# Joint logits of the two key kinds in half of the first attention, with later yields, a later lambda and another raw copy

## The chip, the cores and the metric

The kernel runs on one core of a Trainium2 chip. The metric is the device time of one execution in microseconds (us). The kernel before takes 1781.61 us (median of three runs, 1781.35 to 1781.64). The core has five engines that work in parallel: TensorE (PE; its weight loads are the row PEld), VectorE (DVE), ScalarE (ACT), GpSimd (POOL) and SyncE (SP, which issues most DMAs). Each takes its own instructions strictly in the order in which the program issued them; semaphores make one wait for another. Matmul results land in PSUM, in banks of 128 x 512 fp32.

## The reference

A trunk of two layers, sequence 512, model width 1024, fp32. Cut to what the change touches:

```python
q_rot = rope(q, positions); k_slc = rope(k_slc, positions); k_win = rope(k_win, positions)
def block(i):                                   # 128 queries
    logit_c = einsum('btghd,bngd->bghtn', qg, kc) * scale      # compressed keys, unrotated q
    p_c = masked_softmax(logit_c, cmp_end <= t)
    logit_s = einsum('btghd,bgtkd->bghtk', qrg, ks) * scale    # "selected" keys
    p_s = masked_softmax(logit_s, kpos <= t)
    logit_w = einsum('btghd,bkgd->bghtk', qrg, kw) * scale     # "window" keys
    p_w = masked_softmax(logit_w, mask_w)
    return gb[..., 0:1] * (p_c @ vc) + gb[..., 1:2] * (p_s @ vs) + gb[..., 2:3] * (p_w @ vw)
lam = exp(sum(lq1 * lk1)) - exp(sum(lq2 * lk2)) + lambda_init  # for the second, differential attention
h = rmsnorm(x); proj = h @ w_in                                # the dense part, and so on to the FFN
```

With 512 positions, 16 selected blocks of 64 and a window of 512, both the selected and the window attention come to plain causal attention, each with its own keys and values. The first attention has 8 heads of width 64 in two groups g; a group shares its keys. The second (differential) attention needs the scalar `lam`; a gMLP (`sgu`) is the third mixer. All three are merged by gates, and an FFN follows.

## The kernel before

**The dense products** (input projection, merge, FFN) are the bulk of PE's work. Each fp32 product is made as three products of split operands (high x high, low x high, high x low), L184 to L186 with 512 columns each, or L224 to L226 in the token-major form `tm`. Weights arrive by DMA; ACT rounds them to the high part (L163, `wh`), DVE or POOL subtracts for the low part (L166, `wl`). Every dense chunk takes one of three PSUM banks `g`, and the next chunk but two must wait until the evacuation of that bank has ended.

**The small work** (aux work) is woven in. `layer_tasks` lists the dense tasks, `aux_tasks` two lanes of generators: lane X with `tables` (sines and cosines, and before the change the lambdas too), `cmp_aux` (compression MLP), `sgu_aux` and `cmp_soft` (softmax over compressed keys, for g = 0 and 1, parts A and B), lane Y with `nsa` (first attention) and `diff` (second). In `run`, each dense step yields a cost in ns; a lane gets that much credit and `step` runs it to its next yield, which charges its own price. So a larger yielded number sets everything behind it later in program order, on every engine's queue at once. `later(n, f)` sets f back by n such steps; `D_OA` holds the three delays of the first attention's output: the sum `fin` (L963), the rounding `hi_` (ACT, L969) and the low part `lo_` (L972). The program is fixed when it is built; nothing moves at run time.

**The first attention**, `nsa(g)`, goes over 32 units: pairs of heads hp, halves of the queries, key kinds (0 selected, 1 window), query tile i of the half, head h. For each unit `sA` makes logits in one of two banks `s` (`logits`, L871 and L872: high and low part of the keys, (i+1)*128 columns), DVE masks and takes the row maximum (L860), ACT exponentiates (L862). `sN` normalises (DVE L898, POOL L902), `sB` transposes on PE into one of two banks `t` (L919), ACT and DVE split the result (L920, L928), `sC` multiplies with the values (L941) into bank `o`. The rotated keys of all four (kind, g) pairs lie in `KR`, two tiles, one for a kind.

**Rotary embedding** of the queries (`rope_pair`): the halves of a projection are multiplied out of PSUM by DVE (L659, L660 and L669, L670), and for `QA0`, `QA1` a raw copy is kept for the compressed attention (ACT, L664 and L672). Only when the last reader has ended does the bank come free. After `QA1` the values `V` follow in the dense order (L224 to L226 with 280 columns).

Of the kernel before, what the change touches and what calls it, by code (L numbers as in the profile page):

```python
# [15 lines left out]
AF = mybir.ActivationFunctionType  # L16
# [5 lines left out]
P, TT, KT, FT = 128, 4, 8, 22  # L22
# [3 lines left out]
QA, KC, VC, KS, VS, KW, VW, GA, QB, KB, VB, UU, VV = (  # L26
    0, 512, 640, 768, 896, 1024, 1152, 1280, 1304, 1816, 2328, 2840, 3352)
# [3 lines left out]
D_ROPE = (1500, 3500, 11000, 18000, 24000, 33000)  # L31
D_MX, D_ACT, D_OA, D_XP = (2, 4), (7, 19), (1, 4, 17), 2
D_NORM = (10, 13)
# [47 lines left out]
class Kern:  # L81
# [287 lines left out]
    def setup2(self):  # L369

        nc = self.nc
# [13 lines left out]
        for j in range(2):  # L385
            a = sm(f"a{j}")
# [10 lines left out]
        c = 1 / (2 * pi)  # L397
        cs = []
        e = 18
        for _ in range(4):  # L400
            q = Fraction(int(c * 2 ** e), 2 ** e)
# [4 lines left out]
        k = sm("k")  # L406
        f = sm("f")
# [23 lines left out]
        for j, off in enumerate((0.25, 0.0)):  # L431
            w = sm("w")
# [5 lines left out]
            d = sm("d")  # L438
# [6 lines left out]
        for j, tab in enumerate((self.cosT, self.sinT)):  # L445
            for h in range(4):
                nc.sync.dma_start(tab[32 * h:32 * h + 32, :], tab_d[j].rearrange("a b c -> a (b c)"))
        yield
        first = len(nc.cur_bb.bb.instructions)
        lq = self.lq.rearrange("p (l f d) -> p l f d", l=L, f=4)  # L450
        self.nlam, self.bh, self.sub = [], [], []
        for l in range(L):
            li = 0.8 - 0.6 * math.exp(-0.3 * l)
            ex = self.const(f"ex{l}", [P, 2])
# [15 lines left out]
        self.holds.append((first, len(nc.cur_bb.bb.instructions)))  # L470
        yield

# [123 lines left out]
    def cmp_aux(self, which):  # L596
        nc = self.nc
        ps = self.hid[which]
# [5 lines left out]
        nc.scalar.activation(hg[0:64], hg[0:64], AF.Gelu_apprx_tanh)  # L604
        yield 4500
        pt = self.bank("t", [P, 2, 64])
# [4 lines left out]
        if which == "k":  # L611
# [4 lines left out]
            for ab in range(2):  # L616
                for k in range(2):
                    c0 = (k * 2 + ab) * P
                    nc.tensor.matmul(pk[:, ab, :], w2[:, c0:c0 + P], hT[:, k, :],
                                     start=(k == 0), stop=(k == 1))  # L620
# [31 lines left out]
    def rope_pair(self, name, raw=None):  # L652
# [13 lines left out]
        def fb(ps):  # L666
# [4 lines left out]
            if raw is not None:  # L671
                nc.scalar.activation(st["raw"][:, 1, :], ps, AF.Copy)  # L672
            o1, o2 = st["t1"], st["t4"]
# [62 lines left out]
    def sgu_aux(self):  # L736
# [40 lines left out]
        norm(0)  # L777
        yield 650
        pss, tmps = {}, {}
# [14 lines left out]
    def cmp_soft(self, g, part):  # L794
# [54 lines left out]

        for w, f in (((1300, s0), (1300, s1), (2600, s2), (2600, ex)), ((2600, s3), (2600, s4), (1300, s5)))[part]:  # L850
            f()
            yield w
# [12 lines left out]
    def logits(self, q, k, kl, i):  # L865

        nc = self.nc
        n = (i + 1) * P
        ts = slice(i * P, (i + 1) * P)
        s = self.bank("s")  # L870
        nc.tensor.matmul(s[:, :n], q[:, ts], k[:, :n], start=True, stop=False)  # L871
        nc.tensor.matmul(s[:, :n], q[:, ts], kl[:, :n], start=False, stop=True)  # L872
        return s

    def nsa(self, g):
# [3 lines left out]
        units = [(2 * hp + h, half, kind, 2 * half + ii) for hp in range(2) for half in range(2)  # L879
                 for kind in range(2) for ii in range(2) for h in range(2)]  # L880
        E, PT, OB, LO = {}, {}, {}, []
        st = {}

        def sA(u):
            hh, half, kind, i = units[u]
            s = self.logits(q2[hh // 2][:, hh % 2], kh[kind][:, g], kl[kind][:, g], i)
            if u % 2 == 0:
                st["sm"] = self.small("sm2", 2, 5)
            E[u] = self.soft(s, (i + 1) * P, i, st["sm"][:, u % 2:u % 2 + 1])[0], st["sm"]
# [109 lines left out]
    def diff(self, p):  # L999
# [6 lines left out]
        def sA(u, j):  # L1006
            c, i = units[u]
            s = self.logits(q2[c][:, j], kh[c][:, j], kl[c][:, j], i)
            E[u, j] = self.soft(s, (i + 1) * P, i)
# [132 lines left out]
    def merge_tasks(self, add, l, br, first, last, need, lead=1):  # L1142
        def gate(i0, m):
            if last and m == 0:
                for c in range(4):
                    self.load_x(self.xsrc, c)
            yield from self.fm(i0, [self.gate_evac(br, m)], self.xg)

        def branch(i0, m):
            x = {"a": self.oa, "b": self.ob, "c": self.oc}[br]  # L1150
            yield from self.fm(i0, [self.br_evac(br, m, first, last)], x, K=4)
            if m == 7 and last:
                self.ensure("mx")
        B = br.upper()
        for m in range(8 + lead):
            if m < 8:
                add("g%s%d" % (B, m), [("g" + br, m)], lambda i0, m=m: gate(i0, m))
            if m >= lead:
                add("b%s%d" % (B, m - lead), [("b" + br, m - lead)], lambda i0, m=m: branch(i0, m - lead), need=need)
# [142 lines left out]
    def layer_tasks(self, l):  # L1302
# [103 lines left out]
        add("V", [("v", c) for c in range(3)], g_v)  # L1406
        self.merge_tasks(add, l, "c", True, False, ["sgu"])
        add("KB0", [("KB0", "A"), ("KB0", "B")], g_rope("KB0"), need=["rows1"])
# [34 lines left out]
    def aux_tasks(self, l):  # L1443
# [7 lines left out]
        X.append(("sgu", ["vv%d" % l], self.sgu_aux))  # L1451
        X.append(("softA0", ["QA0%d" % l], lambda: self.cmp_soft(0, 0)))
        X.append(("cmpv", ["wv3%d" % l], lambda: self.cmp_aux("v")))
        X.append(("softB0", ["V%d" % l], lambda: self.cmp_soft(0, 1)))
# [17 lines left out]
    def run(self):  # L1472
# [3 lines left out]
        lanes = [[], []]  # L1476
        tag = lambda n, l: n if n == "tables" else n + str(l)
        for l in range(L):
# [57 lines left out]
def pack(inp):  # L1536
# [9 lines left out]
    for l in range(L):  # L1546
        w = w_in[l]
        groups = {"KR": [KS, KS + 64, KW, KW + 64]}
        for g in range(2):
# [89 lines left out]
```

## Time and profile before

| | |
|---|---|
| median of three runs | 1781.61 us |
| profiled execution | 1781.37 us |
| its span (first to last instruction) | 1779.6 us |
| PE busy | 1761.8 us (99%), 8500 matmuls |
| PEld, DVE, ACT, POOL busy | 83%, 54%, 42%, 20% |
| PE's longest waits in total | ACT raw 2.2, DVE nm 1.9, ACT hg 1.9, POOL e 1.2 us |

About 1.8 us of the profiled execution lie outside its span. A busy PE is not a PE at its best pace: the end of a matmul is modelled, so its cost in a stream is read as the distance from its start to the next start. The order of the instructions on each engine comes from the program and not from the trace.

### The profile page before, as it was taken

What the parts mean: (1) busy time and instruction counts of PE and PEld (TensorE: products, weight loads), DVE (VectorE), ACT (ScalarE), POOL (GpSimd) and SP (SyncE); (2) the same over time, 40 slices, a digit from 0 to 9 for tenths busy, and PEclk for the clock granted to TensorE, in tenths of its full rate; (3) what the DMA queues carried; (4) which work ended last, traced back from release to release, by engine and by line L of the source; (5) the groups of instructions that cost most, each with busy time, mean ns of one, the idle gap of its engine ahead of it and who ended that gap; (6) DMA issues with size and microseconds to landing.
All of it is one profiled execution on the core that took longest, in us unless ns stands there. A gap on an engine that the chain in (4) does not pass through costs nothing. (4 is left out here: it accounts for less than half of the span.)

```text
span 1779.6 us, 22826 instructions
## 1 busy us (share of the span) xinstructions
PE 1761.8 (99%) x8500; PEld 1470.8 (83%) x8500; DVE 968.7 (54%) x1772; ACT 752.9 (42%) x1320; POOL 352.4 (20%) x355
## 2 busy tenths in 40 slices
PE   9999999999999999999999999999999999999998
PEld 7888888888888888888888888888888888888887
DVE  6786674665644444433366676746656444444222
ACT  6456673444433332222234576634444332332222
POOL 0234331444120000000012343315440200000000
PEclk9999999999999999999999999999999999999999
DMA  7571116532222222223344711165323232222221
GB/s 260 180 224 69 54 60 195 172 107 100 105 104 92 98 95 95 95 102 124 106 147 139 222 42 60 69 191 156 141 71 110 92 109 102 97 95 95 95 102 52
DMA packets 67726, 205.78 MB, mean 116 GB/s; under 512 B 8992, under 2 KB 9376, under 8 KB 67616
## 3 DMA queue, kind: packets, MB, share of 16 engines
q1 hardware_dynamic: 67472, 204.29, 34.0%
q8 instruction: 67, 1.10, 0.2%
q14 instruction: 43, 0.35, 0.1%
q10 hardware_dynamic: 144, 0.04, 0.0%
HBM read 185.29 MB, written 19.01 MB: 115 GB/s over the span
## 5 line engine op out<-in xcount | busy, mean ns | idle before, releaser
L163 ACT ACTIVATE wh<-wr 128x1024 fp32r<-128x1024 f32 (+2 forms) x320 | 315.4, 989 | 658.6 <-PE ps_g L186 355.8
L184 PE MATMUL ps_g<-xg,wh 128*128 128x512 f32 x1400 | 555.9, 397 | 0.2
L185 PE MATMUL ps_g<-xg,wl 128*128 128x512 f32 x1400 | 546.2, 390 | 0.3 <-DVE wl L166 0.3
L186 PE MATMUL ps_g<-xg,wh 128*128 128x512 f32 x1400 | 546.4, 390 | 0.1
L166 DVE TENSOR_TENSOR wl<-wr,wh 128x1024 fp32r<-128x1024 f32 (+1 forms) x308 | 366.0, 1190 | 238.0 <-ACT wh L163 237.3
L186 PEld LDWEIGHTS ps_g<-xg,wh 128*128 128x128 f32 x1400 | 262.8, 188 | 56.5 <-DVE xg L283 1.0
L185 PEld LDWEIGHTS ps_g<-xg,wl 128*128 128x128 f32 x1400 | 263.4, 188 | 48.6 <-DVE wl L166 0.6
L184 PEld LDWEIGHTS ps_g<-xg,wh 128*128 128x128 f32 x1400 | 263.1, 188 | 48.9 <-ACT xg L280 1.0
L862 ACT ACTIVATE e<-e,nm 128x128 f32<-128x128 f32 (+1 forms) x192 | 107.5, 560 | 102.3 <-DVE nm L860 95.3
L184 PE MATMUL ps_g<-act,wh 128*128 128x512 f32 (+1 forms) x374 | 141.2, 378 | 0.0
L185 PE MATMUL ps_g<-act,wl 128*128 128x512 f32 (+1 forms) x374 | 140.8, 376 | 0.0
L186 PE MATMUL ps_g<-act,wh 128*128 128x512 f32 (+1 forms) x374 | 140.8, 376 | 0.0
L493 POOL TENSOR_TENSOR acc<-acc,sq 128x512 f32<-128x512 f32 x18 | 29.3, 1629 | 433.6 <-ACT sq L492 433.6
L860 DVE CUSTOM_DVE_ANT_0 e<-ps_s,con 128x128 f32<-128x128 f32 (+1 forms) x192 | 92.2, 483 | 26.6 <-PE ps_s L872 21.9
L902 POOL TENSOR_SCALAR e<-e,sm,ga 128x256 f32<-128x256 f32 (+3 forms) x128 | 82.0, 653 | 119.6 <-DVE sm L898 107.3
L1184 DVE TENSOR_TENSOR fb<-ps_g,R 128x512 f32<-128x512 f32 x44 | 30.4, 692 | 129.1 <-PE ps_g L186 129.1
L166 POOL TENSOR_TENSOR wl<-wr,wh 128x512 fp32r<-128x512 f32 x48 | 73.4, 1530 | 118.8 <-ACT wh L163 118.8
L1175 DVE TENSOR_TENSOR fa<-ps_g,R 128x512 f32<-128x512 f32 x44 | 30.4, 692 | 95.3 <-PE ps_g L186 95.3
L184 PEld LDWEIGHTS ps_g<-act,wh 128*128 128x128 f32 x374 | 70.3, 188 | 13.0
L186 PEld LDWEIGHTS ps_g<-act,wh 128*128 128x128 f32 x374 | 70.3, 188 | 13.0
L185 PEld LDWEIGHTS ps_g<-act,wl 128*128 128x128 f32 x374 | 70.4, 188 | 12.7
L1227 POOL TENSOR_TENSOR acc<-acc,sq 128x512 f32<-128x512 f32 x5 | 6.9, 1382 | 316.6 <-ACT sq L1225 316.6
(248 smaller groups left out, 2548.1 us busy)
## 6 DMA issues: line engine op xcount, KB each, us to landing
wr<-in_wst SPq DMA_DIRECT2D x266, 512.0 KB, 3.3
rp_d<-pc SPq DMA_DIRECT2D x112, 128.0 KB, 3.4
wr<-in_wst SPq DMA_DIRECT2D x52, 256.0 KB, 2.6
q<-rp_d SPq DMA_DIRECT2D x16, 512.0 KB, 5.5
kh<-rp_d SPq DMA_DIRECT2D x24, 256.0 KB, 6.0
xT<-in_xT SPq DMA_DIRECT2D x7, 512.0 KB, 5.8
kl<-rp_d SPq DMA_DIRECT2D x12, 256.0 KB, 6.9
xtok<-in_xtok SPq DMA_DIRECT2D x4, 512.0 KB, 8.8
```

The lines of the kernel that those rows point to most:

```text
L163: nc.scalar.activation(h[:, :w], t[:, :w], AF.Copy)
L166: eng.tensor_tensor(lo[:, a:b], t[:, a:b], h[:, a:b].bitcast(F32), op=OP.subtract)
L184: nc.tensor.matmul(out, wh[:, c], xh[:, ts], start=first, stop=False)
L185: nc.tensor.matmul(out, wl[:, c], xh[:, ts], start=False, stop=False)
L186: nc.tensor.matmul(out, wh[:, c], xl[:, ts], start=False, stop=last)
L493: (nc.vector if k == KT - 1 else nc.gpsimd).tensor_tensor(self.acc, self.acc, sq, op=OP.add)
L860: nc.vector.tensor_tensor_reduce(out=e[:, :n], in0=s[:, :n], in1=self.mask[:, S - n:], scale=-0.125, scalar=3e38, op0=OP.add, op1=OP.min, ...
L862: nc.scalar.activation(e[:, :n], e[:, :n], AF.Exp, bias=nm, scale=-1.0, accum_out=sm)
L902: nc.gpsimd.tensor_scalar(e[:, :n], e[:, :n], sm[:, h:h + 1], self.ga[:, i, b:b + 1], op0=OP.mult, op1=OP.mult)
L1175: self.nc.vector.tensor_tensor(t, ps, self.R, op=OP.mult)
L1184: nc.vector.tensor_tensor(t, ps, self.R, op=OP.mult)
L1227: (nc.vector if k == KT - 2 else nc.gpsimd).tensor_tensor(self.acc[:, ts], self.acc[:, ts], sq[:, ts], op=OP.add)
```

## The change

It has four parts.

- **Joint logits.** The columns of `KR` are put in another order, so that one tile holds both kinds of one group. For half 0 (query tiles 0 and 1) one pair of products covers both kinds: 256 columns instead of two pairs of 128 for tile 0, 512 instead of two pairs of 256 for tile 1. The second kind's softmax reads the other half of the same bank later. In half 0 the units run kind by kind within a tile. Over two layers and two groups, 32 pairs of 128 columns and 32 of 256 become 16 of 256 and 16 of 512: 64 matmuls fewer. Half 1 is as it was.
- **Later traces.** `D_OA` goes from (1, 4, 17) to (3, 6, 17); `cmp_aux` for the keys of layer 0 yields 6500 instead of 4500 before its transposes; `sgu_aux` yields 1950 instead of 650 after its first norm; `cmp_soft` of group 0 gets an empty first stage of 2600, and its `s2` yields 1300 instead of 2600.
- **Lambda order.** The lambdas leave `tables` and become an aux task of their own behind `softA0`; gate tasks no longer wait for the mixer, and the merge of mixer c also needs the lambdas.
- **Raw copy.** The second raw copy of `QA1` is made by DVE instead of ACT.

```diff
-D_MX, D_ACT, D_OA, D_XP = (2, 4), (7, 19), (1, 4, 17), 2
+D_MX, D_ACT, D_OA, D_XP = (2, 4), (7, 19), (3, 6, 17), 2
...
+    def lambdas(self):
...
-        yield
+        yield 300
...
-        yield 4500
+        yield 6500 if which == "k" and self.l == 0 else 4500
...
             if raw is not None:
-                nc.scalar.activation(st["raw"][:, 1, :], ps, AF.Copy)
+                if raw == 0:
+                    nc.scalar.activation(st["raw"][:, 1, :], ps, AF.Copy)
+                else:
+                    nc.vector.tensor_copy(st["raw"][:, 1, :], ps)
...
         norm(0)
-        yield 650
+        yield 1950
...
-        for w, f in (((1300, s0), (1300, s1), (2600, s2), (2600, ex)), ((2600, s3), (2600, s4), (1300, s5)))[part]:
+        for w, f in (((2600 * (g == 0), lambda: None), (1300, s0), (1300, s1), (1300, s2), (2600, ex)), ((2600, s3), (2600, s4), (1300, s5)))[part]:
...
-        n = (i + 1) * P
         ts = slice(i * P, (i + 1) * P)
         s = self.bank("s")
-        nc.tensor.matmul(s[:, :n], q[:, ts], k[:, :n], start=True, stop=False)
-        nc.tensor.matmul(s[:, :n], q[:, ts], kl[:, :n], start=False, stop=True)
+        o = s[:, :(i + 1) * P] if len(k.shape) == 2 else s[:, :2 * (i + 1) * P].rearrange("p (a n) -> p a n", a=2)
+        nc.tensor.matmul(o, q[:, ts], k, start=True, stop=False)
+        nc.tensor.matmul(o, q[:, ts], kl, start=False, stop=True)
         return s
...
-                 for kind in range(2) for ii in range(2) for h in range(2)]
+                 for kind, ii in ([(0, 0), (1, 0), (0, 1), (1, 1)], [(0, 0), (0, 1), (1, 0), (1, 1)])[half]
+                 for h in range(2)]
...
-            s = self.logits(q2[hh // 2][:, hh % 2], kh[kind][:, g], kl[kind][:, g], i)
+            if half:
+                s = self.logits(q, kh[g][:, kind, :n], kl[g][:, kind, :n], i)
+            elif kind == 0:
+                s = self.logits(q, kh[g][:, :, :n], kl[g][:, :, :n], i)
+                st["s", u % 2] = s[:, n:]
+            else:
+                s = st["s", u % 2]
...
-                add("g%s%d" % (B, m), [("g" + br, m)], lambda i0, m=m: gate(i0, m))
+                add("g%s%d" % (B, m), [("g" + br, m)], lambda i0, m=m: gate(i0, m), need=need[1:])
...
-        self.merge_tasks(add, l, "c", True, False, ["sgu"])
+        self.merge_tasks(add, l, "c", True, False, ["sgu", "lambda"])
...
         X.append(("softA0", ["QA0%d" % l], lambda: self.cmp_soft(0, 0)))
+        if l == 0:
+            X.append(("lambda", [], self.lambdas))
...
-        groups = {"KR": [KS, KS + 64, KW, KW + 64]}
+        groups = {"KR": [KS, KW, KS + 64, KW + 64]}
```

In the program after, a line behind the inserted code has a higher number than in the program before: the `hg` activation L604 is L608 there, the two exponentials L460 are L464, the softmax step L860 is L867, the sum L963 is L980.

**ACT, layer 0, around the first compression MLP.** `ang` is the argument of the sine tables, `ex` the lambdas' exponentials, `ctmp` and `hg` the hidden layer of the MLP, which PE then transposes. Before:

```order
L441 ACT_TABLE_LOAD
L441 ACTIVATE ang<-ang 128x128 x2
L460 ACT_TABLE_LOAD
L460 ACTIVATE ex_600<-ex_600 128x2
L460 ACTIVATE ex_611<-ex_611 128x2
L600 ACTIVATE ctmp<-ps_s 64x256
L163 ACTIVATE wh<-wr 128x1024
L604 ACT_TABLE_LOAD
L604 ACTIVATE hg<-hg 64x256
```

After:

```order
L604 ACTIVATE ctmp<-ps_s 64x256
L441 ACT_TABLE_LOAD
L441 ACTIVATE ang<-ang 128x128 x2
L608 ACT_TABLE_LOAD
L608 ACTIVATE hg<-hg 64x256
L163 ACTIVATE wh<-wr 128x1024
```

`ctmp` stands ahead of the sines now, and the exponentials with their table load are gone from in front of `hg`. On PE the two transposes that read `hg` stand five dense products later than before.

**DVE, layer 0, end of `QA1`'s evacuation** (`t` products of the rotation, `raw` the raw copy, `hg` the other compression MLP). Before:

```order
L660 TENSOR_TENSOR t_1061<-ps_g,sinR 128x512
L603 TENSOR_TENSOR hg<-ps_s,ctmp 64x256
L166 TENSOR_TENSOR wl<-wr,wh 128x840
L669 TENSOR_TENSOR t_1123<-ps_g,sinR 128x512
L670 TENSOR_TENSOR t_1124<-ps_g,cosR 128x512
L166 TENSOR_TENSOR wl<-wr,wh 128x840
```

After (the last of the fourteen lambda rows that stand between L166 and L673):

```order
L469 TENSOR_SCALAR bh_1096<-par_64 128x24
L472 TENSOR_SCALAR sub_1098<-par_64 128x1
L461 ISA junk,ex_1089<-lq 128x64
L461 ISA ex_1089 128x1
L466 SCALAR_TENSOR_TENSOR nl_1083<-ex_1078 128x1
L466 SCALAR_TENSOR_TENSOR nl_1094<-ex_1089 128x1
L673 TENSOR_TENSOR t_1120<-ps_g,sinR 128x512
L674 TENSOR_TENSOR t_1121<-ps_g,cosR 128x512
L679 COPY raw<-ps_g 128x512
L607 TENSOR_TENSOR hg<-ps_s,ctmp 64x256
```

The lambdas' fourteen DVE instructions, two of which wait for ACT's exponentials, moved in front of the three readers of `QA1`'s bank; `hg` moved behind them. In layer 1 the same place holds no lambda.

**DVE, first attention of group 0, start of the half with tiles 2 and 3** (`ce`, `cmx`, `csm` belong to the compressed softmax of group 1, `oa` to the output of an earlier pair of heads). Before:

```order
L822 TENSOR_TENSOR ce<-ce,cmx 128x512
L860 ISA e,nm<-ps_s,con 128x256
L860 ISA nm 128x1
L830 TENSOR_REDUCE csm<-ce 128x16
L831 RECIPROCAL csm<-csm 128x16
L963 TENSOR_TENSOR oa<-oa,otmp 128x512
L898 RECIPROCAL sm_1805<-sm_1805 128x2
L834 TENSOR_TENSOR csm<-csm,ga 128x16
L836 TENSOR_TENSOR csm<-csm,con 128x16
L928 TENSOR_TENSOR pt<-ps_t,pt 128x4x128
L860 ISA e,nm<-ps_s,con 128x384
L860 ISA nm 128x1
```

After:

```order
L829 TENSOR_TENSOR ce<-ce,cmx 128x512
L980 TENSOR_TENSOR oa<-oa,otmp 128x512
L945 TENSOR_TENSOR pt<-ps_t,pt 128x2x128
L867 ISA e,nm<-ps_s,con 128x384
L867 ISA nm 128x1
L989 TENSOR_TENSOR oa<-oa 128x512
L837 TENSOR_REDUCE csm<-ce 128x16
L867 ISA e,nm<-ps_s,con 128x384
L867 ISA nm 128x1
L838 RECIPROCAL csm<-csm 128x16
```

The first softmax step of 384 columns stood behind six other instructions after the reduction over `ce`; now it stands ahead of that reduction.

## Rows read from the trace of the kernel before

**Rows 1.** Page, busy time (share of the span) and instructions of PE
```profile
PE 1761.8 (99%) x8500; PEld 1470.8 (83%) x8500; DVE 968.7 (54%) x1772; ACT 752.9 (42%) x1320; POOL 352.4 (20%) x355
```
**Rows 2.** Waits of PE: line, releaser; us in total, times, longest
```profile
PE ps_g L224 <- ACT raw L672: 2.2, 2, 1.1
PE ps_s L871 <- DVE nm L860: 1.9, 2, 0.9
PE ps_t L608 <- ACT hg L604: 1.9, 1, 1.9
...
PE ps_t L919 <- POOL e L902: 1.2, 2, 0.6
...
PE ps_t L805 <- ACT raw L672: 0.9, 2, 0.6
...
PE ps_s L757 <- DVE v L752: 0.3, 1, 0.3
```
**Rows 3.** Timeline of PE, pair of 128 columns: start, us, instruction [idle <-releaser]
```profile
130.43 0.22 PE L871 MATMUL ps_s<-kh,q 128*128 128x128 f32 x1
...
130.60 0.45 PE L184 MATMUL ps_g<-xg,wh 128*128 128x512 f32 x1
130.88 0.39 PE L185 MATMUL ps_g<-xg,wl 128*128 128x512 f32 x1
```
**Rows 4.** Timeline of PE, a pair of 256, then a pair of 512
```profile
172.75 0.28 PE L871 MATMUL ps_s<-kh,q 128*128 128x256 f32 x1
...
173.00 0.40 PE L184 MATMUL ps_g<-xg,wh 128*128 128x512 f32 x1
173.23 0.40 PE L185 MATMUL ps_g<-xg,wl 128*128 128x512 f32 x1
...
250.60 0.40 PE L871 MATMUL ps_s<-kh,q 128*128 128x512 f32 x1
...
251.06 0.49 PE L919 MATMUL ps_t<-con,e 128*128 128x128 f32 x3
```
**Rows 5.** Groups of PE by line and shape: xcount, busy us, mean ns
```profile
L941 PE MATMUL ps_o<-pt,v 128*128 128x256 f32 x64 | 12.7, 280 | 0.0
```
**Rows 6.** Timeline of PE at the transposes of `hg`, layer 0
```profile
66.70 0.35 PE L608 MATMUL ps_t<-con,hg 64*128 64x64 f32 x2 [1.86 <-ACT hg L604]
```
**Rows 7.** Windows: from:to, length, busy (x count), granted PE clock, DMA
```profile
66.90:70.40 3.50, 3.50 (x10) 2.74 (x9) 0.29 (x1) 1.73 (x3) 1.84 (x2) 0.51 0.60 177
118.00:119.50 1.50, 1.47 (x10) 1.33 (x10) 1.50 (x1) 0.21 (x1) 1.44 (x2) 1.00 0.70 234
```
**Rows 8.** Timeline of ACT ahead of `hg`, layer 0
```profile
61.64 0.31 ACT L441 ACTIVATE ang<-ang 128x128 f32<-128x128 f32 x1 [0.73 <-DVE ang L440]
61.97 1.28 ACT L460 ACT_TABLE_LOAD   x1
63.27 0.30 ACT L460 ACTIVATE ex<-ex 128x2 f32<-128x2 f32 x2
```
**Rows 9.** Timeline of PE, ACT and DVE at `V`'s third bank, layer 0
```profile
118.03 0.40 PE L224 MATMUL ps_g<-wh,xg 128*128 128x280 f32 x1 [1.11 <-ACT raw L672]
...
117.40 0.57 ACT L672 ACTIVATE raw<-ps_g 128x512 f32<-128x512 f32 x1
...
113.58 0.42 DVE L603 TENSOR_TENSOR hg<-ps_s,ctmp 64x256 f32<-64x256 f32 x1 [1.25 <-ACT ctmp L600]
...
115.33 0.68 DVE L669 TENSOR_TENSOR t<-ps_g,sinR 128x512 f32<-128x512 f32 x1
115.93 0.68 DVE L670 TENSOR_TENSOR t<-ps_g,cosR 128x512 f32<-128x512 f32 x1
```
**Rows 10.** Timeline of DVE, the first lambda instruction
```profile
60.20 0.22 DVE L457 CUSTOM_DVE_ANT_0 junk<-lq 128x64 f32<-128x64 f32 x1
```
**Rows 11.** Timeline of DVE and PE, first attention, start of tiles 2 and 3
```profile
176.46 0.69 DVE L963 TENSOR_TENSOR oa<-oa,otmp 128x512 f32<-128x512 f32 x1 [0.47 <-ACT otmp L960]
...
178.93 0.50 PE L871 MATMUL ps_s<-kh,q 128*128 128x512 f32 x1 [0.93 <-DVE nm L860]
```

More of the change, by code (lines that the diff above doesn't have):

```diff
@@ L448, in setup2 @@
         yield
+    def lambdas(self):
+        nc = self.nc
         first = len(nc.cur_bb.bb.instructions)
@@ L885, in sA @@
             hh, half, kind, i = units[u]
-            s = self.logits(q2[hh // 2][:, hh % 2], kh[kind][:, g], kl[kind][:, g], i)
+            n = (i + 1) * P
+            q = q2[hh // 2][:, hh % 2]
+            if half:
[5 more added lines that the diff above has]
+                s = st["s", u % 2]
             if u % 2 == 0:
@@ L1007, in sA @@
             c, i = units[u]
-            s = self.logits(q2[c][:, j], kh[c][:, j], kl[c][:, j], i)
+            n = (i + 1) * P
+            s = self.logits(q2[c][:, j], kh[c][:, j, :n], kl[c][:, j, :n], i)
             E[u, j] = self.soft(s, (i + 1) * P, i)
@@ L1476, in run @@
         lanes = [[], []]
-        tag = lambda n, l: n if n == "tables" else n + str(l)
+        tag = lambda n, l: n if n in ("tables", "lambda") else n + str(l)
         for l in range(L):
```

## The prediction, made before the changed kernel was run

> **What bounds the kernel now.** I read the busy shares first. PE is busy for 1761.8 of 1779.6 us, so nothing else can shorten the kernel by much: what counts is fewer or cheaper matmuls, and the places where PE stands still [rows 1]. Next come PE's waits, which give those places by line. DVE, at 54%, is far from full on average, but each engine works in order, so one step that waits holds up a PSUM bank that stands behind it. The largest waits are 2.2, 1.9, 1.9, 1.2 and 0.9 us [rows 2], and the edits touch the instructions around each of them. The last views were timelines around these places, one window for the clock, and the order of the instructions before and after.
>
> **The change part by part.** The sum is made against the profiled execution, 1781.37 us, which is 0.24 us under the median of the three runs.
>
> *Joint logits.* A pair of 128 columns starts at 130.43, and the second dense product behind it, L185, at 130.88, where a dense product of 512 columns alone takes 0.23: the pair costs 0.45 − 0.23 = 0.22 us, though its columns are only half of a dense product's [rows 3]. A pair of 256 columns takes 173.23 − 172.75 − 0.23 = 0.25 us by the same count, and a pair of 512 takes 251.06 − 250.60 = 0.46 us [rows 4]. For tile 0, two pairs of 128 (0.44) become one of 256 (0.25): 0.19 to 0.22 us each, with the rounding of the rows, sixteen times, 3.3 us. For tile 1 two of 256 (0.50) become one of 512 (0.46), sixteen times 0.02 to 0.04, 0.4 us. Together 3.7 us. The new moving operand has two pieces a tile apart in memory. No logits row shows that, but the value product L941 reads two pieces of 128 columns, and its mean of 280 ns is that of the plain 256-column logits, 0.28 [rows 4, 5]; so I take no price for it. Bounds: 0 if a pair in pieces cost 0.44, and 4.5 us if tile 1 also saved 0.06.
>
> The 0.22 us of the small pair is the row on which this term hangs. The Trainium skill, "TensorE: Matmul & The Clock Gate", section "Back-to-back issue gap", gives an isolated matmul N/2.4 + 2.5 ns, 56 ns for 128 columns and 109 for 256. By that four small products and two joint ones cost nearly the same, and the joining would save some 0.1 us over the whole kernel. The trace doesn't agree for the pair: it takes 0.22 us here, not 0.11, as the section itself warns for streams in which weight loads share the pace.
>
> *`hg` in layer 0.* PE stands still for 1.86 us until `hg` is there [rows 6], and then runs 3.50 us with a granted clock of 0.51, the lower of its two levels (1.2 GHz), having stood still just before [rows 7]. At the upper level that work takes about 1.8 us, so the stop costs 1.86 + 1.7 = 3.6 us. After, the sines end where they did, at 61.95; then the exponentials with their table load (1.28 and 0.30) are not in front of `hg` any more [rows 8]. `hg` needs its own table load, 1.28, and the activation, 0.4, and can end at some 63.6 (DVE adds it earlier, since `ctmp` stands ahead of the sines). PE wants it five products later than before, at 64.84 + 5 × 0.23 = 66.0 (64.84 is where the wait began). That leaves 2.4 us of room: −3.6 us. What is late next is nothing on ACT: the weight split that it passes is one step of 1 us that now runs behind `hg`. Bounds: 0 if `hg` is late by as much, −3.7.
>
> *Raw copies.* The compressed softmax waits 0.9 us in two places for the first raw copy [rows 2]. The empty stage sets its matmuls four or more dense products back, 0.9 us; the longer wait was 0.6. I take −0.8.
>
> `V`'s third bank waits 1.11 us in each layer for the second raw copy, which ACT makes at 117.40 behind a table load, though DVE's last reader L670 started at 115.93; the bank was wanted at 118.03 − 1.11 = 116.92 [rows 9]. In layer 1 DVE does it at once: L669 can start some 0.3 earlier, since `hg` (0.42) is behind it, then two steps of 0.60 and a copy of about the same length give 115.05 + 1.8 = 116.9 on the scale of layer 0. The wait goes, −1.1. In layer 0 the lambdas stand between. The first of them takes 0.22 [rows 10]; four like it and eight smaller ones come to an estimated 0.9, since their ends overlap; then the exponential, 0.30 [rows 8], and the two last ones, together as long as the first. So 115.05 + 0.9 + 0.5 + 1.8 = 118.3, and the wait is 1.4 instead of 1.1, +0.3 us. Both layers: −0.8. Bounds: −2.2 if ACT's exponentials slip into DVE's earlier work, +2.9 if the wait comes to 2 us and the clock falls as it did behind the 1.86 us of `hg` (+0.9 longer in layer 0, +1.7 for the clock, and nothing won in layer 1 but 0.3 lost).
>
> *Later traces of the first attention.* At the start of tiles 2 and 3 the logits wait 0.93 us in each layer for the row maximum of 384 columns (1.9 in all) [rows 2, 11]. DVE was held before it by L963 at 176.46, which waits for ACT, whose own copies stood behind a step of the compressed softmax. After, the row maximum has only one split and the sum in front of it; the reduction over `ce` and the five other steps behind which it stood are no longer there, an estimated 1.6 us by the one of 0.69 [rows 11] among them, and 0.93 is enough. −1.9. What is queued behind is the compressed softmax of group 1, whose products have until the merge. The waits for POOL's normalising, 1.2 us in two places [rows 2], are in the dense stretch without filler; the order leaves the reader about as far behind its logits as it needs, so I take half, −0.6, bounds −1.2 and 0.
>
> *The gMLP in layer 1.* The wait of 0.3 for `v` [rows 2] goes with the longer yield: −0.3.
>
> *New waits.* The lane of the first attention starts about three products later, and has to be empty at the same task; the joint bank makes rounds without logits on PE and others with the double. I can't place such waits, and price them by the small ones of the list, 0.3 each [rows 2]: two per layer, +1.2, from 0 to +4.
>
> Sum: −3.7 − 3.6 − 0.8 − 0.8 − 1.9 − 0.6 − 0.3 + 1.2 = −10.5, so 1781.4 − 10.5 = **1770.9 us**.
>
> **The rivals.**
>
> *Only the product counts.* The waits removed come back one bank further on. For it speaks that all edits besides the product merely reorder, and PE's queue can only wait where work is late; against it that ACT and DVE are idle for much of these stretches, so there is room. −3.7 and nothing else but the clock's 1.7, which needs a long stop: 1776.0 to 1777.7, 1777 in the middle.
>
> *The lambdas stop `V` for 2 us.* As bounded above, the clock falls in layer 0: against the sum +0.6 of wait and +1.7 of clock, and 1773.2. For it speaks that two of the fourteen wait for another engine in order; against it that the stop of 1.11 us left the clock at 1.00, the upper level (2.4 GHz) [rows 7, 9], and that my count gives 1.4.
>
> *The joint bank blocks.* The second kind's row maximum reads the bank late, and DVE has other work in front of it, so each later pair of logits finds both `s` banks taken. By the row of 0.93 us [rows 11] a group of heads and tiles pays 0.9; with 16 such groups in both layers 14.4 us, which makes −10.5 into +3.9, 1785.3. It turns slower from 12 blocked groups on. For it speaks that the bank's life grows by one round; against it that in the order the next logits into that bank also stand one round later, so the distance from the release to the next use is as it was.
>
> *The product in pieces is no faster,* nor any other product: then 1774.6.
>
> **How the numbers follow.** Forecast 0.62, with its own range from 1768 to 1773.5. Only the product counts 0.10, lambdas with the clock 0.13, product in pieces no faster 0.09, joint bank 0.06. The range takes the first four: 1767 (the lower bounds of `hg`, POOL's wait and the raw copies, without the new waits) to 1777; outside are the joint bank and the tails, some 0.15. What a measurement of this kernel tells from no change is 0.2%, 3.6 us. Faster, under 1778: 0.91, the sum without the joint bank and a third of the first rival's spread. The joint bank gives 0.03 between the bounds and 0.03 beyond; so same 0.06, slower 0.03.
>
> **What would show it.** Right: 64 matmuls fewer in the page and a joint pair that costs 0.25; no wait for `hg` and a granted clock of 1.00 after it; no wait on the row maximum at the start of tiles 2 and 3; `V`'s wait gone in layer 1 and about 1.4 us in layer 0, put down to DVE instead of ACT. Wrong: a second stretch at the lower clock, near `V` in layer 0; waits of logits on the row maximum in the first half, in every group; or a 256-column pair that takes 0.4 us.

## The result and the profile after

The changed kernel takes 1770.22 us (median of four runs, 1770.12 to 1771.77), the kernel before on the same chip 1781.48. The ratio is 0.9944, 95% interval 0.9931 to 0.9957: faster by 11 us (0.6%), against 10.7 forecast. The profiled execution takes 1770.18 us, its span 1768.3. One of the four runs lies 1.5 us above the other three, and the runs of the kernel before come in two groups too (1779.3 to 1780.4 and 1781.0 to 1782.5 us): this fits a fall of the granted clock, worth 1.7 us, that comes in some executions of a kernel and not in others (last section), so a difference between medians can hold up to that much.

PE's busy line answers to [rows 1]:

```profile
PE 1755.5 (99%) x8436; PEld 1465.0 (83%) x8436; DVE 968.9 (55%) x1774; ACT 751.4 (42%) x1317; POOL 354.0 (20%) x355
```

There are 64 matmuls fewer. PE's waits (line, releaser; us in total, times, longest) answer to [rows 2]:

```profile
PE ps_g L224 <- DVE raw L679: 2.5, 2, 1.9
...
PE ps_t L936 <- DVE pcT L855: 0.9, 2, 0.4
PE ps_s L764 <- DVE stmp L770: 0.6, 1, 0.6
```

The waits on `nm`, on `hg`, on POOL's `e`, on the first raw copy and on `v` are gone; `V`'s wait has grown from 2.2 to 2.5; `pcT` (compressed softmax, which holds a bank `t`) and `stmp` (gMLP) are new. The waits of before, start and end of the program left out, come to 8.7 us with 0.3 for `wl`, which is gone too; those of after to 4.0. A joint pair, in PE's timeline (start, us, instruction), answers to [rows 3, 4]:

```profile
129.60 0.28 PE L878 MATMUL ps_s<-kh,q 128*128 128x256 f32 x1
...
129.83 0.40 PE L184 MATMUL ps_g<-xg,wh 128*128 128x512 f32 x1
130.06 0.40 PE L185 MATMUL ps_g<-xg,wl 128*128 128x512 f32 x1
```

It costs 130.06 − 129.60 − 0.23 = 0.23 us, though its moving operand lies in two pieces. The place of `hg`, in PE's and ACT's timelines and by a window (length, busy, granted clock), answers to [rows 6 to 8]:

```profile
66.24 0.33 PE L612 MATMUL ps_t<-con,hg 64*128 64x64 f32 x2
...
63.14 0.31 ACT L441 ACTIVATE ang<-ang 128x128 f32<-128x128 f32 x1 [0.87 <-DVE ang L440]
63.47 1.28 ACT L608 ACT_TABLE_LOAD   x1
64.77 0.42 ACT L608 ACTIVATE hg<-hg 64x256 f32<-64x256 f32 x1
...
66.90:70.40 3.50, 3.50 (x26) 3.22 (x24) 1.23 (x3) 3.30 (x5) 0.19 (x1) 1.00 0.39 112
```

No wait, and the clock is up at 1.00 where it was 0.51. But `hg` ended at 65.19, not at the forecast 63.6. `V`'s third bank in both layers, and DVE in front of it in layer 0 (timelines), answer to [rows 9, 10]:

```profile
116.54 0.40 PE L224 MATMUL ps_g<-wh,xg 128*128 128x280 f32 x1 [1.94 <-DVE raw L679]
...
990.01 0.40 PE L224 MATMUL ps_g<-wh,xg 128*128 128x280 f32 x1 [0.55 <-DVE raw L679]
...
112.36 1.03 DVE L166 TENSOR_TENSOR wl<-wr,wh 128x840 fp32r<-128x840 f32 x1 [1.64 <-ACT wh L163]
113.31 0.22 DVE L461 CUSTOM_DVE_ANT_0 junk<-lq 128x64 f32<-128x64 f32 x1
...
114.53 0.16 DVE L466 SCALAR_TENSOR_TENSOR nl<-ex 128x1 f32<-128x1 f32 x1 [0.20 <-ACT ex L464]
114.61 0.68 DVE L673 TENSOR_TENSOR t<-ps_g,sinR 128x512 f32<-128x512 f32 x1
...
115.81 0.68 DVE L679 COPY raw<-ps_g 128x512 f32<-128x512 f32 x1
```

The lambdas take DVE from 113.31 to 114.61, 1.3 us, as worked out. The wait is longer than forecast because L166 itself starts late, after 1.64 us of waiting for ACT.

In sum, from the two profiled executions: 4.7 us less of listed waits, 1.7 us of clock, and 3.1 us of matmuls (experiment 9) make 9.5 of the 11.3 us by which the spans differ. The other 1.8 us were not placed.

### The profile page after: what moved, and what is told of

Read it like the earlier page. It is cut to its first block, busy times and chain, and to the rows that moved or that the text cites. A ratio compares the mean times of both kernels' runs of the same rounds, so it can differ in the third digit from the quotient of the medians.

```text
span 1768.3 us, 22696 instructions
## 1 busy us (share of the span) xinstructions
PE 1755.5 (99%) x8436; PEld 1465.0 (83%) x8436; DVE 968.9 (55%) x1774; ACT 751.4 (42%) x1317; POOL 354.0 (20%) x355
## 4 chain that ended last, share of the span: by engine, by line
PE 97%; DVE 1%; ACT 1%; DMA 0%; issue 0%; POOL 0%; SPq 0%; DVEq 0%; ACTq 0%; POOLq 0%
PE ps_g L184 26%; PE ps_g L185 26%; PE ps_g L186 26%; PE ps_o L958 2%; PE ps_t L936 2%; PE ps_s L879 2%; PE ps_g L224 2%; PE ps_s L878 2%; PE ps_g L225 2%; PE ps_g L226 2%; PE ps_o L1061 1%; DVE wl L166 1%; PE ps_o L226 1%; PE ps_o L224 1%; PE ps_o L225 0%; PE ps_t L1050 0%
## 5 line engine op out<-in xcount | busy, mean ns | idle before, releaser
L166 DVE TENSOR_TENSOR wl<-wr,wh 128x1024 fp32r<-128x1024 f32 (+1 forms) x308 | 367.5, 1195 | 234.8 <-ACT wh L163 231.3
L869 ACT ACTIVATE e<-e,nm 128x384 f32<-128x384 f32 (+2 forms) x192 | 107.2, 559 | 89.0 <-DVE nm L867 85.0
L497 POOL TENSOR_TENSOR acc<-acc,sq 128x512 f32<-128x512 f32 x18 | 29.3, 1626 | 433.6 <-ACT sq L496 433.6
L919 POOL TENSOR_SCALAR e<-e,sm,ga 128x128 f32<-128x128 f32 (+3 forms) x128 | 82.1, 652 | 111.8 <-DVE sm L915 88.7
L867 DVE CUSTOM_DVE_ANT_0 e<-ps_s,con 128x384 f32<-128x384 f32 (+2 forms) x192 | 90.8, 483 | 22.3 <-PE ps_s L879 20.7
L166 POOL TENSOR_TENSOR wl<-wr,wh 128x512 fp32r<-128x512 f32 x48 | 72.6, 1513 | 117.7 <-ACT wh L163 117.7
L945 DVE TENSOR_TENSOR pt<-ps_t,pt 128x512 fp32r<-128x512 f32 (+1 forms) x96 | 56.7, 597 | 27.4 <-ACT pt L937 27.2
```

What stands on the lines that cost most here:

```text
L166: eng.tensor_tensor(lo[:, a:b], t[:, a:b], h[:, a:b].bitcast(F32), op=OP.subtract)
L867: nc.vector.tensor_tensor_reduce(out=e[:, :n], in0=s[:, :n], in1=self.mask[:, S - n:], scale=-0.125, scalar=3e38, op0=OP.add, op1=OP.min, ...
L869: nc.scalar.activation(e[:, :n], e[:, :n], AF.Exp, bias=nm, scale=-1.0, accum_out=sm)
L919: nc.gpsimd.tensor_scalar(e[:, :n], e[:, :n], sm[:, h:h + 1], self.ga[:, i, b:b + 1], op0=OP.mult, op1=OP.mult)
L945: nc.vector.tensor_tensor(lo, pt, hi.bitcast(F32), op=OP.subtract)
```

## The experiments

All times are medians of at least five runs. The kernel before lay between 1779.3 and 1782.5 us beside them, the changed kernel at 1770.2; ratios are to the kernel before on the same chip. The waits come from one profiled execution of each; those at the start and the end of the program, which differ by up to 1 us between executions, are left out. In the cuts of code, three dots stand for lines left out.

**1. The product alone.** Before, with the new `logits`, `sA`, `units` and column order, and nothing else.

```diff
 D_MX, D_ACT, D_OA, D_XP = (2, 4), (7, 19), (1, 4, 17), 2
...
-        groups = {"KR": [KS, KS + 64, KW, KW + 64]}
+        groups = {"KR": [KS, KW, KS + 64, KW + 64]}
```

> The kernel before with the joint logits alone (other column order of KR, other unit order in half 0, one product for both kinds); the yields, the lambdas and the raw copy as before. Theory: the product gives 16 x 0.21 + 16 x 0.03 = 3.7 us and nothing else moves, so about 1777.8 us; the wait for hg (1.86 us) with its stretch at the lower clock, V's waits of 1.11 us and the waits of the logits on the row maximum of 0.93 us stay. Rival 1: a joint pair in pieces costs two pairs, 1781.4 us. Rival 2: the joint bank blocks, 0.9 us in each of 16 groups, 1785 us or more.

1772.38 us, ratio 0.996 (0.9946 to 0.9973), about 7.6 us faster than before and not 3.7. PE's waits (columns as above):

```profile
PE ps_g L224 <- ACT raw L672: 2.2, 2, 1.1
PE ps_t L608 <- ACT hg L604: 1.7, 1, 1.7
...
```

The waits of the first attention, 1.9 on `nm` and 1.2 on POOL's `e` [rows 2], are not in the list any more, though every trace is as early as before. So it was the joint logits that removed them.

**2. Everything but the product.** The changed kernel with the old logits, units and column order.

```diff
...
-                 for kind, ii in ([(0, 0), (1, 0), (0, 1), (1, 1)], [(0, 0), (0, 1), (1, 0), (1, 1)])[half]
-                 for h in range(2)]
+                 for kind in range(2) for ii in range(2) for h in range(2)]
...
```

> The changed kernel with the joint logits undone (column order, unit order and logits of the kernel before); later traces, lambda order and raw copy as changed. Theory: the parts add up, so 1770.2 + 3.7 = 1773.9 us. Rival: the joint bank's empty rounds are what frees DVE and removes the logits' waits on the row maximum; then these come back, 2 x 0.93 us more, and it is 1775.8 us.

1776.96 us, ratio 0.9981 (0.9973 to 0.999). Undoing the product costs 6.7 us, with these waits of the first attention back:

```profile
PE ps_s L878 <- DVE nm L867: 0.9, 2, 0.4
PE ps_t L926 <- POOL e L909: 0.8, 2, 0.4
```

The rival was right in kind. The later traces halve the wait on `nm`; they don't remove it. In this profiled execution the granted clock also falls behind `V`'s wait in layer 0, 1.91 us, as it does not in that of the changed kernel (window: length, busy, granted clock):

```profile
116.20:119.60 3.40, 3.40 (x15) 3.40 (x16) 1.07 (x2) 3.18 (x5) 3.17 (x3) 0.50 0.84 234
```

So part of the 6.7 us may be the clock; between the lowest runs, 1775.84 and 1770.12 us, undoing the product costs 5.7.

**3. The lambdas behind the second compression MLP.**

```diff
-        if l == 0:
-            X.append(("lambda", [], self.lambdas))
         X.append(("cmpv", ["wv3%d" % l], lambda: self.cmp_aux("v")))
+        if l == 0:
+            X.append(("lambda", [], self.lambdas))
```

> The changed kernel with the lambda task behind the second compression MLP (cmpv) instead of in front of it, so that no lambda stands ahead of QA1's evacuation. Theory: the lambdas are the larger half of V's wait in layer 0; it falls from 1.94 us to the 0.55 us of layer 1, and the time to 1768.8 us. Rival 1: the wait is the later compressed softmax and the copy, not the lambdas; it stays near 1.9 us and 1770.2 us. Rival 2: the exponentials now stand in front of the first attention's softmax and hold its logits; the wait moves there, 1770.2 us or more.

1770.72 us (1770.5 to 1770.87), ratio 0.9946 (0.9934 to 0.9959): no gain. PE's waits:

```profile
PE ps_g L224 <- DVE raw L679: 1.1, 2, 0.6
...
PE ps_t L849 <- DVE ce L844: 0.7, 1, 0.7
...
PE ps_s L878 <- DVE nm L867: 0.4, 1, 0.4
PE ps_s L878 <- DVE nl L466: 0.3, 1, 0.3
```

`V`'s wait in layer 0 falls to 0.60, as the theory had it, and 1.4 us come back in the first attention and its compressed softmax (`ce`; `nl` is the lambda itself), as rival 2 had it.

**4. The raw copy back on ACT.**

```diff
-                if raw == 0:
-                    nc.scalar.activation(st["raw"][:, 1, :], ps, AF.Copy)
-                else:
-                    nc.vector.tensor_copy(st["raw"][:, 1, :], ps)
+                nc.scalar.activation(st["raw"][:, 1, :], ps, AF.Copy)
```

> The changed kernel with QA1's second raw copy back on ACT; the rest as changed. Theory: the copy on DVE stands behind two products of 0.60 us, while ACT, whose table load now comes later than the copy, could make it at the same time; V's wait falls by 0.5 to 0.6 us in each layer, to 1.35 and 0, and the time to 1769.1 us. Rival: ACT gets to the copy as late as in the kernel before, the waits are 1.1 us or more in both layers and the time is 1770.2 us or above.

1769.96 us (1769.82 to 1771.93), ratio 0.9945 (0.9932 to 0.9957), and `V` waits 1.93 and 0.53 us, as with DVE. My theory fell. ACT's timeline in layer 1:

```profile
989.49 0.90 ACT L163 ACTIVATE wh<-wr 128x840 fp32r<-128x840 f32 x1
991.00 0.60 ACT L676 ACTIVATE raw<-ps_g 128x512 f32<-128x512 f32 x1 [0.61 <-DVE t L674]
991.61 1.28 ACT L608 ACT_TABLE_LOAD   x1
```

ACT is free in time and then waits until DVE has done its last product out of the bank: the copy is made after DVE's reads on either engine. The Trainium skill, "PSUM — Partial Sum Buffer", section "PSUM bank collisions raise a hardware error", says that the compiler adds a dependency between any two instructions on different engines that touch the same part of a bank, reads and writes alike. The trace agrees: ACT waits 0.61 us for DVE's read. This profiled execution took 1771.93 us, the other four 1769.8 to 1770.4; in it the clock falls behind `V`'s stop of 1.93 us:

```profile
118.30:121.70 3.40, 3.40 (x16) 3.02 (x15) 1.35 (x2) 2.17 (x4) 1.64 (x2) 0.50 0.90 251
```

**5. The yield of 6500 back at 4500.**

```diff
-        yield 6500 if which == "k" and self.l == 0 else 4500
+        yield 4500
```

> The changed kernel with the compression MLP's yield back at 4500, so that PE reads hg five dense products earlier. Theory: what removed the wait for hg is the table load and the exponentials that left ACT's queue in front of it; hg ends at 65.2 us and would be wanted at 66.2 - 1.1 = 65.1, so a wait of 0.1 to 0.3 us, the clock stays up, 1770.2 to 1770.5 us. Rival: the later transposes did it; the wait is above 1 us and the clock falls, 1772 us or more.

1772.56 us (1771.02 to 1774.39), ratio 0.9953 (0.994 to 0.9965). The theory fell; PE's timeline:

```profile
64.84 0.33 PE L612 MATMUL ps_t<-con,hg 64*128 64x64 f32 x2 [1.45 <-ACT hg L608]
```

Without the later transposes 1.45 of the 1.86 us are back, with no exponential and no second table load in front of `hg`. The clock does not fall behind this stop, but 54 us later, behind `V`'s of 1.88 us:

```profile
119.00:122.40 3.40, 3.40 (x16) 3.02 (x15) 0.08 (x1) 2.58 (x5) 1.84 (x2) 0.50 0.84 263
```

So of the 2.3 us above the changed kernel some 1.7 are the clock at `V`, and the wait for `hg` adds less than its length: the lowest run is 0.9 us above the changed kernel's.

**6. The lambdas back behind the tables,** with the yield of 6500.

```diff
+        yield from self.lambdas()
...
-        self.merge_tasks(add, l, "c", True, False, ["sgu", "lambda"])
+        self.merge_tasks(add, l, "c", True, False, ["sgu"])
```

> The changed kernel with the lambdas back behind the tables (gates no longer wait for them), the rest as changed, with the yield of 6500. Theory: hg ends 1.6 us later, at 66.8 against 66.2 wanted, a wait of 0.6 us, too short for the clock; V's wait in layer 0 falls from 1.94 to the 0.55 us of layer 1; 1769.4 us. Rival: the wait for hg comes back whole and the clock falls, 1.9 + 1.6 - 1.4 = 2.1 us more, 1772.3 us.

1770.75 us (1770.58 to 1770.96), ratio 0.9943 (0.9929 to 0.9956). The wait for `hg` is 0.07 us and `V`'s 0.25 in layer 0, but the gMLP pays:

```profile
PE ps_s L765 <- DVE stmp L771: 0.8, 1, 0.8
PE ps_s L765 <- DVE v L760: 0.8, 1, 0.8
PE ps_g L224 <- DVE raw L680: 0.8, 2, 0.5
PE ps_g L185 <- DVE wl L166: 0.5, 1, 0.5
```

So the lambda order gave at most 0.5 us by itself.

**7. The lambdas in front of the gMLP.**

```diff
+        if l == 0:
+            X.append(("lambda", [], self.lambdas))
         X.append(("sgu", ["vv%d" % l], self.sgu_aux))
         X.append(("softA0", ["QA0%d" % l], lambda: self.cmp_soft(0, 0)))
-        if l == 0:
-            X.append(("lambda", [], self.lambdas))
```

> The changed kernel with the lambda task in front of the gMLP (sgu), where ACT has little to do; the table of the exponentials is then loaded there and not in front of the compressed softmax of group 0. Theory: ACT's split of V's weights comes 1.3 us earlier in layer 0 and no lambda stands in front of QA1's evacuation, so V's wait in layer 0 goes from 1.94 to 0, layer 1 keeps its 0.55; nothing moves to the first attention; 1768.2 us. Rival 1: the lambdas push the gMLP, whose wait of 0.64 us for stmp grows by a us; 1769.2 us. Rival 2: V's wait depends on the second product of the rotation alone and stays above 0.5 us; 1768.8 us.

1768.70 us (1768.45 to 1769.67), ratio 0.9932 (0.992 to 0.9945): faster than the changed kernel, whose runs don't reach down to 1769.7 (the intervals of the two ratios overlap, the runs don't). The gain is 1.5 us of the forecast 2.0. PE's waits:

```profile
PE ps_g L224 <- DVE raw L679: 0.5, 1, 0.5
...
PE ps_s L764 <- DVE v L759: 0.4, 1, 0.4
```

Only layer 1 of `V` is left, and 0.4 for `v` is new, the start of rival 1.

**8. No later traces.**

```diff
-D_MX, D_ACT, D_OA, D_XP = (2, 4), (7, 19), (3, 6, 17), 2
+D_MX, D_ACT, D_OA, D_XP = (2, 4), (7, 19), (1, 4, 17), 2
```

and likewise 4500, 650, no empty stage, 2600 behind `s2`.

> The changed kernel with all later traces undone (delays 1, 4, 17; yields 4500, 650; no empty stage, 2600 behind s2); joint logits, lambda order and raw copy as changed. Theory, after the joint product alone had already removed the logits' and POOL's waits: the traces are worth little; the waits for the first raw copy come back (1.3 us), the gMLP's in layer 1 too (0.7), while V's waits shrink by 0.6 us in each layer, and the new waits for pcT (1.4) and stmp (1.1) go; 1769.1 us. Rival: the traces carry the gain that the joint product does not, some 3 us, and it is 1773 us.

1773.65 us (1773.39 to 1776.18), ratio 0.9962 (0.9949 to 0.9974): the traces are worth 3.4 us together, the rival's figure, and these are their places:

```profile
PE ps_t L612 <- ACT hg L608: 1.3, 1, 1.3
PE ps_s L764 <- DVE v L759: 1.3, 2, 1.0
PE ps_t L812 <- ACT raw L677: 1.3, 2, 0.6
...
PE ps_g L224 <- DVE raw L679: 0.9, 2, 0.5
```

`hg`, the gMLP and the first raw copy, none of them in the first attention. `V`'s waits are 0.51 and 0.35 here instead of 1.94 and 0.55.

**9. Two products into one bank.** The changed kernel, with its order of units, and each joint pair made as two pairs again.

```diff
-        nc.tensor.matmul(o, q[:, ts], k, start=True, stop=False)
-        nc.tensor.matmul(o, q[:, ts], kl, start=False, stop=True)
+        for a in ([slice(None)] if len(k.shape) == 2 else [0, 1]):
+            oa, ka, la = (o, k, kl) if len(k.shape) == 2 else (o[:, a], k[:, a], kl[:, a])
+            nc.tensor.matmul(oa, q[:, ts], ka, start=True, stop=False)
+            nc.tensor.matmul(oa, q[:, ts], la, start=False, stop=True)
```

> The changed kernel with everything in place (order of units, one bank for both kinds, all other edits), only the joint product is made as two pairs again, one for each kind, into the two halves of the bank. It parts the matmuls saved from the order of the units. Theory: the matmuls are worth 3.7 us and the order of the units the other 3.1 us of what undoing both cost (6.8 us); so 1770.2 + 3.7 = 1773.9 us, without waits of logits on the row maximum or of the transposes on POOL. Rival 1: the matmuls carry it all, 1777.0 us. Rival 2: a joint pair in pieces saves nothing and the order carries it all, 1770.2 us.

1774.48 us (1773.23 to 1775.54), ratio 0.9964 (0.9952 to 0.9977). The theory holds: 4.3 us by the medians, 3.1 by the spans of the profiled executions (1771.4 and 1768.3), neither of which has a fall of the clock at `V` or `hg`. No wait on `nm` and none on POOL's `e` is in its list. Experiment 2 lies another 2.5 us higher by the medians and 2.6 by the lowest runs: that is what the order of the units and the shared bank are worth together here; they were not parted. Four small products in PE's timeline:

```profile
129.19 0.22 PE L880 MATMUL ps_s<-kh,q 128*128 128x128 f32 x1
129.25 0.28 PE L881 MATMUL ps_s<-kl,q 128*128 128x128 f32 x1
129.36 0.27 PE L880 MATMUL ps_s<-kh,q 128*128 128x128 f32 x1
129.47 0.27 PE L881 MATMUL ps_s<-kl,q 128*128 128x128 f32 x1
129.58 0.45 PE L184 MATMUL ps_g<-xg,wh 128*128 128x512 f32 x1
129.87 0.40 PE L185 MATMUL ps_g<-xg,wl 128*128 128x512 f32 x1
```

129.87 − 129.19 − 0.23 = 0.45 us, against 0.23 for the joint pair: 0.22 us, sixteen times 3.5.

**10. The stop at `hg` restored:** the edits of 5 and 6 together.

> The changed kernel with the lambdas back behind the tables and the compression MLP's yield back at 4500, so that the stop at hg stands as in the kernel before and all else is changed. Theory: the stop alone is 1.9 us more than with the yield of 6500 (1770.75 us), and the clock falls behind it in most executions, 1.6 us more: 1772.6 without and 1774.2 us with the fall. Rival: the stop falls in the kernel before for another reason; with the changed order it stays under 1 us and the time under 1771.8 us.

1771.08 us (1770.45 to 1772.38), ratio 0.9947 (0.9935 to 0.996). The stop is there, 1.87 us, and the clock falls behind it (window: length, busy, granted clock):

```profile
68.60:70.90 2.30, 2.30 (x7) 1.82 (x6) 0.00 (x0) 0.47 (x1) 1.68 (x2) 0.50 0.72 240
```

The profiled execution took 1772.27 us and one other 1772.38, the three others 1770.5 to 1771.1; no trace of these was kept. The kernel to compare with is that of experiment 6, with the lambdas in the same place and no stop: 1770.75 us. With the fall the stop costs 1.5 us, not the 3.5 of the theory. The gMLP waits 0.1 us instead of 1.6, and the 0.8 for weight halves (`wh` and `wl`) are gone, while `V`'s wait in layer 0 grows from 0.25 to 0.69 and 0.56 for the first raw copy is new. That DVE and ACT catch up while PE stands fits this; it was not tried by itself.

**11. Lambdas early, the old `s2` of group 1, and the table of layer 1 early.** Experiment 7, and

```diff
...
+            w = self.small("wex", 1, 1)
+            self.nc.scalar.activation(w, self.V[3][:, 0:1], AF.Exp)
...
-(1300, s2), (2600, ex)
+(2600 if g else 1300, s2), (2600, ex)
```

> The kernel with the lambda task in front of the gMLP (1768.7 us), and two edits more: the stage s2 of group 1 yields 2600 again (against the waits for pcT of 0.44 us in both layers), and in layer 1 one exponential of a single column stands in front of the gMLP, so that the table is loaded there and not in front of the compressed softmax (against V's wait of 0.5 us in layer 1). Theory: 0.8 and 0.6 us less, 1767.3 us. Rival 1: the table load delays the gMLP's statistics in layer 1 and PE waits there, 0.4 to 0.7 us, 1768.0 us. Rival 2: the waits for pcT come from the later delays of the attention's output and not from s2; they stay, 1768.1 us.

1768.78 us (1768.47 to 1769.28), ratio 0.9933 (0.9919 to 0.9946): no gain over experiment 7. `V` waits in neither layer, but `v` does now in layer 1 too, and the wait for `pcT` has become one for `pt` of the same length:

```profile
PE ps_t L942 <- DVE pt L951: 0.9, 2, 0.4
PE ps_s L770 <- DVE v L765: 0.8, 2, 0.4
...
```

**12. The same with a later gMLP in layer 0.**

```diff
-        yield 1950
+        yield 1950 if l else 3250
```

> The kernel of the run before it in this call, with the gMLP's yield in layer 0 at 3250 instead of 1950, against the gMLP's two waits there (0.36 us for v, 0.65 for stmp). Theory: v is then ready, 0.5 us less; stmp's wait moves with the rest and may stay: 1766.8 us. Rival: what is behind, the softmax of group 0 and QA1's evacuation, comes later too and V waits again, 1767.5 us or more.

1768.60 us (1768.05 to 1769.29), ratio 0.9932 (0.9919 to 0.9944): the wait for `v` in layer 0 goes, the one for `stmp` grows from 0.66 to 0.83, and the compressed softmax waits 0.17. Experiments 7, 11 and 12 are not told apart by their runs; all three beat both kernels, 7 with the smallest edit.

## Why the prediction was right, and where its steps were not

The time was right to 0.7 us and in the range. Of its steps some held, and others only summed to the right figure: as measured, the terms come to 9.5 of the 11.3 us by which the spans differ, so the nearness of the sum is in part luck; what `V` did not give was made up by gains that no term had.

- **Joint logits, −3.7: right in size** (experiment 9: 3.1 by the spans, 4.3 by the medians), with the pair at 0.23 instead of 0.25 us. The "product in pieces" rival is refuted by the pair itself. What the step left out is what the product's order of units does to the waits.
- **Waits of the first attention, −1.9 and −0.6: they went, 3.1 us, for another reason.** I put them down to the later traces, by the order of DVE. Experiment 1 removes both without a later trace; experiment 2 leaves 0.9 and 0.8 with all later traces; experiment 9 shows that the order of units and the shared bank suffice without saving a matmul, with the later traces in place. By what steps they do so was not traced.
- **`hg`, −3.6: gone, but by the yield and not by the table load.** The failing step is "after, the sines end where they did, at 61.95". They ended at 63.45. With the lambdas away, a weight split of DVE moved between the steps of the sines, 1.22 us at 60.57, and ACT waited for it; that ate most of what the exponentials with their table load had given. In the kernel before that split stood behind the last step; DVE's timelines, before and then after:

```profile
60.00 0.28 DVE L412 SCALAR_TENSOR_TENSOR ang<-ang 128x128 f32<-128x128 f32 x1
61.82 1.21 DVE L166 TENSOR_TENSOR wl<-wr,wh 128x1024 fp32r<-128x1024 f32 x1
...
60.37 0.28 DVE L412 SCALAR_TENSOR_TENSOR ang<-ang 128x128 f32<-128x128 f32 x1
60.57 1.22 DVE L166 TENSOR_TENSOR wl<-wr,wh 128x1024 fp32r<-128x1024 f32 x1
...
62.88 0.23 DVE L440 TENSOR_SCALAR ang<-ang 128x128 f32<-128x128 f32 x1
```

Some 0.4 of the 1.5 us is only that the whole execution runs later by then (60.37 against 60.00 for the same step). The room was 66.24 − 65.19 = 1.05 us and not 2.4, and without the yield the wait is 1.45 (experiment 5); with the yield and the lambdas in their old place it is 0.07 (experiment 6). The term was also no net gain of 3.6: restored, the stop with its clock costs 1.5 us against experiment 6, since other waits shrink (experiment 10).

- **First raw copy, −0.8: right in size.** Experiment 8 brings back 1.3 us, but undoes all the later traces at once; that it is the empty stage among them was not tried alone.
- **`V`, −0.8: wrong, it is +0.3.** The lambdas cost 1.3 us and the count from L166 on was right: L673, L674 and the copy are 1.8 us. The failing step is "L669 can start some 0.3 earlier". L166 waited for ACT, whose chain begins with the compressed softmax. In layer 0 its table load starts 5.0 us before `V`'s bank is wanted, against 5.7 in the kernel before and 5.7 in experiment 8: the later traces set it 0.7 us later against `V`, most likely by the empty stage that I had credited under the first raw copy. Undoing all traces brings `V` down to 0.51 and 0.35 us. That DVE could copy sooner than ACT was wrong too: ACT would have waited for DVE.
- **gMLP in layer 1, −0.3: right,** but in layer 0 the wait for `stmp`, 0.6, is new (counted below). It grows to 0.83 when the yield there is raised further (experiment 12).
- **New waits, +1.2: 1.5** (`pcT` 0.9, `stmp` 0.6), in places that I had not named.

Of the rivals, "only the product counts" is half true in a way it did not mean: the joint logits alone bring 7.6 us, the other three parts alone about 3 (experiment 2), and within these the raw copy brings nothing measurable (experiment 4) and the lambda order at most 0.5 us (experiment 6). The joint bank blocked nothing: no wait on `nm` is left. The stop at `V` came, 1.94 us. The fall of the clock that I had tied to it is not in the profiled execution of the changed kernel; with stops of 1.88 to 1.93 us at the same place it is in those of experiments 2, 4 and 5. So that rival was right in part, and more so than my count of 1.4 us.

## What to carry to other kernels

When an edit changes the order in which units go through shared buffers, price the order by itself, by an experiment that keeps the order and undoes the saving: here order and shared bank were some 2.5 of the 5.7 to 6.7 us that undoing the product cost. Before a wait is struck off because something leaves a queue in front of it, ask what will move up into the gap; here a weight split did. And a step that is set later to meet one producer makes everything behind it in its lane later: follow that chain to the next bank before crediting it. And look at the granted clock of every trace behind every long stop: a difference of 1.7 us between two profiled executions can be that alone.

## What the runs showed of the hardware that was not expected

- A stop of PE of about 1.9 us does not by itself decide the clock, nor does its place. The granted clock fell to about half, for 3.4 us, behind 1.86 us (before), 1.68 (experiment 1) and 1.87 (experiment 10) at `hg`, and behind 1.91, 1.93 and 1.88 us at `V` (experiments 2, 4 and 5). Behind 1.94 us at `V` in the changed kernel and 1.92 in experiment 9 it stayed at 1.00 (windows below, in this order). What parts these cases was not tried; one profiled execution of a kernel doesn't show what the clock does in the next.

```profile
116.50:120.50 4.00, 3.96 (x29) 3.74 (x30) 1.82 (x4) 3.60 (x5) 3.35 (x3) 1.00 0.81 273
...
116.20:119.60 3.40, 3.40 (x25) 3.18 (x26) 1.22 (x3) 3.11 (x5) 3.25 (x3) 1.00 0.81 245
```

- Small matmuls of 128 columns cost 0.11 us each, as much as one of 256: a pair of 256 takes 0.23 us, four of 128 take 0.45.
- A moving operand in two pieces streams as fast as one in one piece, 0.23 against 0.25 us for a pair.
